# Splitting POOL's lower parts of weights and reordering a pair's end in the last MLP of a diffusion backbone

## The chip, the cores and the metric

The kernel runs on one core of a Trainium2 chip. The metric is the device time of one execution in microseconds (us), as the median of several runs. Times inside an execution come from one profiled execution; they count from its first instruction.

## The reference

Two layers over 1024 latent tokens and 256 context tokens, model width 1024, all in fp32. Layer 0 mixes tokens with a Conformer convolution module, layer 1 with grouped-query attention; each layer ends in a squared-ReLU MLP. Only the latent tokens are returned, so the MLP of layer 1 runs on 1024 tokens.

```
for i in range(2):
    mod_l = split(silu(c) @ w_mod[i] + b_mod[i], 6)          # shift, scale, gate twice; mod_c alike
    hl, hc = modulate(rms_norm(x, norm1_g[i]), ...), ...
    ol, oc = conv_module(hl), conv_module(hc)   if i == 0    # depthwise convolution of 31 taps
    ol     = gqa_mixer(hl, hc)                  if i == 1    # QK-norm, 2-D rotary, softmax
    xl = xl + mod_l[2] * ol
    hl = modulate(rms_norm(xl, norm2_g[i]), mod_l[3], mod_l[4])
    xl = xl + mod_l[5] * (square(relu(hl @ w_ff1[i])) @ w_ff2[i])    # w_ff1: 1024 x 4096
    ...                                                      # the context likewise in layer 0
return xl
```

## The kernel before

Everything is fp32 in memory. A product is made from split operands: the upper part of a number is its value rounded to the matmul format (fp32r), made by ACT with a copy; the lower part is the value minus its upper part, made by POOL or DVE with a subtraction. Of the four partial products three are kept, so each product of a weight tile and 512 tokens is three matmuls. In `unit`, a 128 x 1024 tile of weights is loaded on SP's queue into a buffer `raw` (three of them), ACT makes its upper part (L205), and POOL (or DVE, where `eng` says so) its lower part in one instruction of 1024 columns (L208).

The language's scheduler places the instructions on the engines. Written order is a preference that `high_priority(n)` moves n instructions ahead; each engine's queue is then worked off strictly in the order in which it was filled, and an instruction that waits holds up what is behind it. A tile with k buffers is handed out again when its last reader is placed before the next writer.

The last MLP (`mlp1`, `ff2`) is written as a Strassen-like scheme with seven products instead of eight for each 2 x 2 block. The token halves and feature halves are combined beforehand into `T1`, `T2`, `T3`, `T4`, `B11`, `B21`, `B22`, each split into upper and lower parts. The 32 column tiles of `w_ff1` are taken as 16 pairs. For pair j, `w1_ops` loads the two raw tiles `ra` and `rb` (L1334, L1335), forms the sums of weights on DVE (L1347 to L1351), splits them (`unit`: L1340 on ACT, L1341 on POOL; `S1`/`S3` in one tile, `S2`/`S4` in another), and splits `A22` on its own (L1354, L1355). All of this is called up 115 instructions ahead for pairs 0 to 7 and 190 for pairs 8 to 15 (`AH1`). There is one buffer for `A22`'s parts.

The loop over pairs then issues on TensorE, twelve matmuls a product (L1186):

- for pairs 8 to 15 A11·B11 into bank b1; for pairs 0 to 7 this and A12·B21 were done before the loop (while the norm was going on) and come back from memory as p1 and s11;
- S1·T1 into b5, copied to p5 (L1376); S3·T3 into b7, copied to p7 (L1380); POOL adds p7 to p5 (L1381); S2·T2 into b6, added to p1 (L1384), and POOL adds p1 to p5 (L1385);
- for pairs 8 to 15 A12·B21 on top of b1, and its hidden values;
- S4·B22 on top of b5: these matmuls add into the bank from which L1376 has copied, so they wait for that copy;
- A22·T4 on top of b7, likewise after L1380.

p1 and p5 lie in a ring of four slots, two for even and two for odd pairs. Then comes the pair's end, which this text calls its tail: the hidden values (ReLU and square, L1299 and L1300, with a store to scratch memory `hd`) of p5; s12 from b5 and p1 (L1395 to L1397); T1 (L1401), T2 (L1403 on POOL), T3 (L1405); p1 from b7 (L1408) and its hidden values; T4 (L1411). T1 to T4 are stored to `hd` by L1400. In the code the part of the tail that needs only S4 stands between S4 and A22, the rest behind A22. `ff2` reads `hd` back and does the second matrix in the same scheme; its `unit` (L1429 ACT, L1430 POOL or DVE) splits 1024 columns at once too.

L251 is the matmul that sums squares over partitions for a norm; it needs DVE's L284, the last addition of the squares.

Of the kernel before, what the change touches and what calls it, by code (L numbers as in the profile page):

```python
# [11 lines left out]
F32 = mybir.dt.float32  # L12
F32R = mybir.dt.float32r
BF16 = mybir.dt.bfloat16
AF = mybir.ActivationFunctionType
ALU = mybir.AluOpType
# [4 lines left out]
P = 128  # L21
# [47 lines left out]


B = [4.0, 3.64, 3.4, 3.6, 0.41]

AHEAD = [80, 60, 130]
UHP = 100
# [45 lines left out]
NPRO = 8  # L120
AH1, AH2 = (115, 190), 200
PB = 2.5
OPS = ("B11", "B21", "T1", "T3", "T2", "B22", "T4")


class Kern:
# [62 lines left out]
    def unit(self, src, eng=None):  # L189

        nc = self.nc
        cols = lambda ts: lambda c, n=1: ts[c * len(ts) // 8][:, c * P % (1024 // len(ts)):][:, :n * P]
        with self.tc.high_priority(self.ahead):
            raw = self.t("raw", [P, 1024], "raw")
            nc.sync.dma_start(out=raw, in_=src)
            self.nu += 1
            if self.six and self.nu % 6 == 0:
                parts = [[self.t(t, [P, 1024 // len(ts)], "wx", F32R) for t in ts] for ts in self.six]
            else:
                w = self.t("w8", [P, 2, 1024], "wsp", F32R)  # L200
                parts = [[w[:, 0]], [w[:, 1]]]
            hi, lo = [cols(ts) for ts in parts]
            n = 8 // len(parts[0])
            for c in range(0, 8, n):
                nc.scalar.activation(hi(c, n), raw[:, c * P:(c + n) * P], AF.Copy)  # L205
            n = 8 // len(parts[1])
            for c in range(0, 8, n):
                (eng or nc.gpsimd).tensor_tensor(lo(c, n), raw[:, c * P:(c + n) * P], hi(c, n).bitcast(F32), ALU.subtract)  # L208
        return hi, lo
# [212 lines left out]
    def mlp(self, i, X, h, N, segs, gates, budget, hook=None, done=None, eng=None, off=False, each=None,  # L422
# [3 lines left out]
        for c in range(NF // CH):  # L426
# [17 lines left out]
            for m2, mn in MGS:  # L444
# [6 lines left out]
                for z in range(mn):  # L451
# [9 lines left out]
                    if done and c == NF // CH - 1:  # L461
                        done(m)
                    self.pump(budget * B[4])
            if hook:
# [156 lines left out]
    def layer0(self):  # L621
# [21 lines left out]
        self.bg = [n1[1], conv[0]]  # L643
        self.pw1(0, B[0], each=lambda: next(pm, None))
        self.drain(n1[1])
        self.bg.insert(0, n1[2])
        self.pw1(1, B[1], each=lambda: next(pm, None))
        self.drain(n1[2])
        n2 = {}

        def mid(ct):
# [3 lines left out]
            if ct == FRONT:  # L655
# [3 lines left out]
                self.bg.insert(0, n2[-1])  # L659
        self.pw1(2, B[2], mid, each=lambda: next(pm, None))  # L660
        self.drain(n2[-1])
# [527 lines left out]
    def stats1(self, X, box):  # L1189
        yield from self.sumsq(lambda k: X[:, k], 512, box, True)  # L1190

    def mlp1(self, at, pre, r0):
        nc = self.nc
        self.ahead, self.six, self.wide = AHEAD[2], None, True
# [46 lines left out]
        for m in range(KT):  # L1241
# [3 lines left out]
            else:  # L1245
                w = self.unit(self.A["wo"][m])
# [50 lines left out]
        def hidden(c, s, j, o):  # L1297

            nc.scalar.activation(s, c, AF.Relu)  # L1299
            nc.scalar.activation(s, s, AF.Square)  # L1300
            nc.sync.dma_start(out=self.hd[OPS.index(o), :, j], in_=s)
# [7 lines left out]
        for j in range(NPRO):  # L1309
            a11, a12 = halves(self.unit(self.A["w1"][1, 2 * j]))  # L1310
            b1 = self.ps("mm", "b1")
            p1 = self.t("tmp", [P, 512], "p1")
# [16 lines left out]
        ring = [work[:, 4 + i] for i in range(4)]  # L1329

        def w1_ops(j):
            with self.tc.high_priority(AH1[j >= NPRO]):
                ra, rb = [self.t("raw", [P, 1024], "raw") for _ in range(2)]
                nc.sync.dma_start(out=ra, in_=self.A["w1"][1, 2 * j])  # L1334
                nc.sync.dma_start(out=rb, in_=self.A["w1"][1, 2 * j + 1])  # L1335
                u = {}

                def unit(names, src, eng):
                    w = self.t("w8", [P, 2, 1024], "wsp", F32R)
                    nc.scalar.activation(w[:, 0], src, AF.Copy)  # L1340
                    eng.tensor_tensor(w[:, 1], src, w[:, 0].bitcast(F32), ALU.subtract)  # L1341
                    for i, n in enumerate(names):
                        u[n] = tuple(lambda k, y=y, i=i: w[:, y, i * 512 + k * P:i * 512 + k * P + P] for y in range(2))
                if j >= NPRO:
                    unit(("A11", "A12"), ra, nc.gpsimd)
                s = lambda i, n=1: work[:, i:i + n].rearrange("p i n -> p (i n)")
                nc.vector.tensor_tensor(s(0), rb[:, 0:512], rb[:, 512:1024], ALU.add)  # L1347
                nc.vector.tensor_tensor(s(1), ra[:, 0:512], rb[:, 0:512], ALU.subtract)
                unit(("S1", "S3"), s(0, 2), nc.gpsimd)
                nc.vector.tensor_tensor(s(2), s(0), ra[:, 0:512], ALU.subtract)  # L1350
                nc.vector.tensor_tensor(s(3), ra[:, 512:1024], s(2), ALU.subtract)  # L1351
                unit(("S2", "S4"), s(2, 2), nc.gpsimd)
                a = self.t("p1", [P, 2, 512], "a22", F32R)
                nc.scalar.activation(a[:, 0], rb[:, 512:1024], AF.Copy)  # L1354
                nc.vector.tensor_tensor(a[:, 1], rb[:, 512:1024], a[:, 0].bitcast(F32), ALU.subtract)  # L1355
                u["A22"] = tuple(lambda k, y=y: a[:, y, k * P:k * P + P] for y in range(2))
            return u

        def bank(i, name):
            return self.ps(("mm", "mm", "mm", "mm", "cv", "cv", "st", "rb")[i], name)  # L1360

        for j in range(NP):
            u = w1_ops(j)
            q = 4 * (j % 2)
            pro = j < NPRO
            p1 = ring[2 * (j % 2)]
            if pro:
                nc.sync.dma_start(out=p1, in_=self.p1d[:, j])
            else:
                b1 = bank(q, "b1")  # L1370
                self.prod(b1, u["A11"], piece("B11"), True)
                nc.scalar.activation(p1, b1, AF.Copy)  # L1372
            b5 = bank(q + 1, "b5")
            self.prod(b5, u["S1"], piece("T1"), True)
            p5 = ring[2 * (j % 2) + 1]
            nc.scalar.activation(p5, b5, AF.Copy)  # L1376
            b7 = bank(q + 2, "b7")
            self.prod(b7, u["S3"], piece("T3"), True)
            p7 = self.t("acc", [P, 512], "p7")
            nc.scalar.activation(p7, b7, AF.Copy)  # L1380
            nc.gpsimd.tensor_tensor(p5, p5, p7, ALU.add)  # L1381
            b6 = bank(q + 3, "b6")
            self.prod(b6, u["S2"], piece("T2"), True)
            nc.vector.tensor_tensor(p1, b6, p1, ALU.add)  # L1384
            nc.gpsimd.tensor_tensor(p5, p5, p1, ALU.add)  # L1385
            s11 = self.t("tmp", [P, 512], "s11")
            if pro:
                nc.sync.dma_start(out=s11, in_=self.hd[OPS.index("B11"), :, j])
            else:
                self.prod(b1, u["A12"], piece("B21"), False)  # L1390
                hidden(b1, s11, j, "B11")
            self.prod(b5, u["S4"], piece("B22"), False)
            hidden(p5, p5, j, "B22")
            s12 = self.t("tmp", [P, 512], "s12")
            nc.vector.tensor_tensor(s12, b5, p1, ALU.add)  # L1395
            nc.scalar.activation(s12, s12, AF.Relu)  # L1396
            nc.scalar.activation(s12, s12, AF.Square)  # L1397
            t1 = self.t("tmp", [P, 512], "t1")
            t2 = self.t("tmp", [P, 512], "t2")
            out = lambda o, s: nc.sync.dma_start(out=self.hd[OPS.index(o), :, j], in_=s)  # L1400
            nc.vector.tensor_tensor(t1, s12, s11, ALU.subtract)  # L1401
            out("T1", t1)
            nc.gpsimd.tensor_tensor(t2, p5, t1, ALU.subtract)  # L1403
            out("T2", t2)
            nc.vector.tensor_tensor(s12, p5, s12, ALU.subtract)  # L1405
            out("T3", s12)
            self.prod(b7, u["A22"], piece("T4"), False)
            nc.vector.tensor_tensor(p1, b7, p1, ALU.add)  # L1408
            hidden(p1, p1, j, "B21")
            t4 = self.t("tmp", [P, 512], "t4")  # L1410
            nc.vector.tensor_tensor(t4, p1, t2, ALU.subtract)  # L1411
            out("T4", t4)
        self.ff2(X)

    def ff2(self, X):


        nc = self.nc
# [7 lines left out]
        def unit(src, eng):  # L1426

            w = self.t("pc", [P, 2, 1024], "u", F32R)
            nc.scalar.activation(w[:, 0], src, AF.Copy)  # L1429
            eng.tensor_tensor(w[:, 1], src, w[:, 0].bitcast(F32), ALU.subtract)  # L1430
            return w

        def add(acc, bank, c):
# [8 lines left out]
        def out(blk, m, x, b):  # L1442

            y = self.t("acc", [P, 512], "y")
            nc.vector.scalar_tensor_tensor(y, b, g[:, m:m + 1], x, ALU.mult, ALU.add)  # L1445
            nc.sync.dma_start(out=self.out[:, m, blk * 512:blk * 512 + 512], in_=y)
# [9 lines left out]
        for c in range(NC):  # L1456
            last = c == NC - 1
# [5 lines left out]
            for what, y, first in ending if last else order:  # L1463
                with self.tc.high_priority(AH2):
                    tu, wu = [], []
                    z = {"B11": 0, "B21": 1, "T4": 3}.get(what)
                    for i in range(2):
                        f = self.t("raw", [P, 1024], "tf")
                        nc.sync.dma_start(out=f.rearrange("p (i n) -> p i n", i=2),
                                          in_=self.hd[OPS.index(what), :, c * CP2 + 2 * i:c * CP2 + 2 * i + 2])  # L1470
                        tu.append(unit(f, V if i else G))
                    for i in range(2):
                        h = slice(1024 * i, 1024 * i + 1024)
                        s = S[:, h]
# [155 lines left out]
```

## Time and profile before

| what | value |
|---|---|
| median of 3 runs | 2923.48 us (2922.95 to 2928.18) |
| profiled execution | 2921.92 us, its span 2920.1 us, granted clock 0.981 |
| PE (TensorE matmuls) | 2759.9 us busy, 95% of the span |
| DVE | 2046.4 us, 70% |
| POOL | 1568.6 us, 54% |
| ACT | 1481.9 us, 51% |
| DMA | 406.66 MB, mean 139 GB/s |

A row of a timeline gives start, duration, engine, line, operation, output and inputs, how many instructions are merged, and in brackets the idle time just before and what ended it. A row of waits gives who waited for whom, the sum in us, how often, and the longest. A row of windows gives the stretch, its length, the busy time (and count) of PE, PEld (weight loads), DVE, ACT and POOL, the granted clock, the DMA share and GB/s. A row of an instruction's line gives the shortest, median and longest duration in ns. SPq is the queue on which loads and stores are issued.

### The profile page before, as it was taken

To read this page: it belongs to the slowest core of one execution; us is meant where nothing else is said; L and a number is where in the kernel's file an instruction comes from. 1 tells how busy PE (TensorE), PEld (TensorE's weight loads), DVE (VectorE), ACT (ScalarE), POOL (GpSimd) and SP (SyncE) were. 2 spreads that over 40 slices of the span, in tenths; PEclk is the share of its full clock that TensorE was granted. 3 is DMA by queue.
4 is the path that set the end of the run, shared out by engine and by line. 5 is a ranking of instruction groups with operands and counts; after the bars stand their busy time and mean duration, and the time that the engine had idled before them with its cause. 6 is when DMAs were issued, how large, how long until landed. Compare 5 with 4: busy or idle time off the path is not lost. (4 is left out here: it accounts for less than half of the span.)

```text
span 2920.1 us, 35997 instructions
## 1 busy us (share of the span) xinstructions
PE 2759.9 (95%) x12634; PEld 2320.2 (79%) x12634; DVE 2046.4 (70%) x3268; ACT 1481.9 (51%) x2386; POOL 1568.6 (54%) x915
## 2 busy tenths in 40 slices
PE   7999999999989999989998899999999888999999
PEld 2778999999888999978886677776767767888887
DVE  3888998987565432455358899976986645558797
ACT  4553554546444354536344576755675544454332
POOL 3777666676456564444334566644666555553221
PEclk9999999999999999999999999999999899999999
DMA  7554333343876534434344411132106454465452
GB/s 239 171 175 160 125 120 115 109 140 120 269 244 202 196 114 157 130 125 141 119 147 144 127 23 22 23 98 61 22 15 217 147 177 160 150 239 190 159 177 101
DMA packets 176580, 406.66 MB, mean 139 GB/s; under 512 B 21328, under 2 KB 64848, under 8 KB 174352
## 3 DMA queue, kind: packets, MB, share of 16 engines
q1 hardware_dynamic: 176400, 404.37, 42.9%
q8 instruction: 99, 1.62, 0.2%
q14 instruction: 81, 0.66, 0.1%
HBM read 343.49 MB, written 60.82 MB: 138 GB/s over the span
## 5 line engine op out<-in xcount | busy, mean ns | idle before, releaser
L208 POOL TENSOR_TENSOR wsp<-raw,wsp 128x1024 fp32r<-128x1024 f32 x254 | 616.8, 2438 | 447.0 <-ACT wsp L205 405.5
L216 PE MATMUL ps<-h,wsp 128*128 128x432 f32 (+1 forms) x2832 | 574.4, 361 | 5.0 <-ACT h L316 2.9
L216 PEld LDWEIGHTS ps<-h,wsp 128*128 128x128 f32 x2832 | 533.3, 189 | 44.4 <-issue 10.1
L205 ACT ACTIVATE wsp<-raw 128x1024 fp32r<-128x1024 f32 x291 | 306.0, 1056 | 316.8 <-PE ps L216 202.7
L554 DVE SCALAR_TENSOR_TENSOR cv<-u,vec,cv 128x464 f32<-128x464 f32 (+2 forms) x696 | 422.7, 669 | 4.8 <-ACT cv L551 3.3
L216 PE MATMUL ps<-hb,wsp 128*128 128x432 f32 (+1 forms) x1920 | 400.4, 363 | 20.1 <-DVE X L459 11.3
L216 PEld LDWEIGHTS ps<-hb,wsp 128*128 128x128 f32 x1920 | 364.1, 191 | 41.6 <-issue 14.6
L1081 POOL TENSOR_TENSOR p<-e,p 128x512 fp32r<-128x512 f32 x223 | 306.6, 1388 | 164.9 <-ACT p L1079 99.5
L1186 PE MATMUL b<-u 128*128 128x512 f32 x1344 | 305.4, 389 | 0.0
L1186 PEld LDWEIGHTS b<-u 128*128 128x128 f32 x1344 | 252.1, 188 | 53.2 <-DVE sums L1437 0.4
L1074 ACT ACTIVATE e<-sT 128x512 f32<-128x512 f32 x320 | 185.8, 595 | 125.3 <-PE sT L1072 105.0
L1036 DVE TENSOR_REDUCE m<-s 128x1 f32<-128x512 f32 (+1 forms) x336 | 191.8, 590 | 11.5 <-PE s L1034 10.0
L1430 POOL TENSOR_TENSOR u<-tf,u 128x1024 fp32r<-128x1024 f32 x28 | 76.7, 2738 | 174.3 <-ACT u L1429 174.3
L459 DVE SCALAR_TENSOR_TENSOR X<-ps,m,X 128x432 f32<-128x432 f32 (+2 forms) x144 | 81.3, 586 | 118.5 <-PE ps L216 118.3
L361 DVE CUSTOM_DVE_ANT_0 rawh<-rawh,scp 128x512 f32<-128x512 f32 x128 | 86.5, 684 | 103.0 <-DMA rawh<-in_wmod 95.6
L1077 DVE CAST p<-e 128x512 fp32r<-128x512 f32 x160 | 116.0, 726 | 31.0 <-ACT e L1074 26.9
L437 DVE TENSOR_TENSOR hb<-ps,hb 128x432 fp32r<-128x432 f32 (+1 forms) x96 | 57.4, 598 | 111.6 <-ACT ps L436 111.4
L1186 PE MATMUL b<-T,wsp 128*128 128x512 f32 x576 | 133.6, 389 | 0.4 <-POOL wsp L1341 0.4
L1088 PE MATMUL O<-p,half 128*128 128x512 f32 x320 | 127.4, 398 | 0.0
L1186 PEld LDWEIGHTS b<-T,wsp 128*128 128x128 f32 x576 | 108.1, 188 | 23.4 <-POOL wsp L1341 0.8
L216 PE MATMUL ps<-h,wx 128*128 128x432 f32 (+1 forms) x624 | 125.4, 356 | 0.0
L208 POOL TENSOR_TENSOR wx<-raw,wx 128x1024 fp32r<-128x1024 f32 x45 | 109.1, 2424 | 27.6 <-ACT wx L205 26.1
(314 smaller groups left out, 5388.6 us busy)
## 6 DMA issues: line engine op xcount, KB each, us to landing
raw<-in_w SPq DMA_DIRECT2D x232, 512.0 KB, 3.4
raw<-in_pw SPq DMA_DIRECT2D x72, 512.0 KB, 3.4
rawh<-in_wmod SPq DMA_DIRECT2D x128, 256.0 KB, 3.6
tf<-hd SPq DMA_DIRECT2D x56, 512.0 KB, 4.0
raw<-in_qkv SPq DMA_DIRECT2D x36, 512.0 KB, 3.3
rawp<-in_wmod SPq DMA_DIRECT2D x32, 512.0 KB, 4.4
raw<-in_w2s SPq DMA_DIRECT2D x16, 1024.0 KB, 7.2
hd<-t SPq DMA_DIRECT2D x48, 256.0 KB, 2.3
```

Source lines behind the costliest of these rows:

```text
L205: nc.scalar.activation(hi(c, n), raw[:, c * P:(c + n) * P], AF.Copy)
L208: (eng or nc.gpsimd).tensor_tensor(lo(c, n), raw[:, c * P:(c + n) * P], hi(c, n).bitcast(F32), ALU.subtract)
L216: self.nc.tensor.matmul(ps, lhsT=(wh, wl, wh)[t], rhs=(ah, ah, al)[t], start=first and i == t == 0, stop=last and i == n - 1 and t == 2)
L361: nc.vector.tensor_tensor_reduce(raw, raw, scp[z], 1.0, 0.0, ALU.mult, ALU.add, accum_out=part[:, z, u:u + 1])
L459: nc.vector.scalar_tensor_tensor(X[:, m, a:a + n], pss[z][:, a:a + n], gates[cc][:, m:m + 1], X[:, m, a:a + n], ALU.mult, ALU.add)
L554: nc.vector.scalar_tensor_tensor(dst, src, tap, acc[z][:, :N], ALU.mult, ALU.add)
L1036: nc.vector.reduce_max(m3[:, qt, j, c:c + 1], s[:, :w], axis=AX.X)
L1074: nc.scalar.activation(e, s, AF.Exp, scale=0.125)
L1077: nc.vector.tensor_copy(p[:, 0], e)
L1081: (nc.vector if u % lm == lm - 1 else nc.gpsimd).tensor_tensor(p[:, 1], e, p[:, 0].bitcast(F32), ALU.subtract)
L1088: nc.tensor.matmul(O[1], lhsT=self.half, rhs=p[:, 0], start=a, stop=False)
L1186: self.nc.tensor.matmul(ps, lhsT=w[t % 2](k), rhs=(ah, ah, al)[t], start=first and k == t == 0, stop=k == 3 and t == 2, skip_group_check=True)
```

## The change

It has four parts. `PLN = 4` makes POOL's lower part in `unit` two instructions of 512 columns instead of one of 1024; DVE's stay whole. A new function `lower` does the same in `w1_ops` and in `ff2`. The raw loads of `w1_ops` are called up 90 instructions further ahead than the rest of it. The tail becomes a function that is called in the next pair, behind the copies p5 and p7 of that pair (the last pair's after the loop); in it L1408's operation stands right behind s12's addition, and A22·T4 follows S4·B22 directly.

```
+PLN = 4
...
-            n = 8 // len(parts[1])
+            n = min(8 // len(parts[1]), 8 if eng else PLN)
             for c in range(0, 8, n):
                 (eng or nc.gpsimd).tensor_tensor(lo(c, n), raw[...], hi(c, n).bitcast(F32), ALU.subtract)
...
+    def lower(self, eng, w, src):
+        n = 512 if eng is self.nc.gpsimd else 1024
+        for i in range(0, 1024, n):
+            eng.tensor_tensor(w[:, 1, i:i + n], src[:, i:i + n], w[:, 0, i:i + n].bitcast(F32), ALU.subtract)
...
         def w1_ops(j):
-            with self.tc.high_priority(AH1[j >= NPRO]):
+            ah = AH1[j >= NPRO]
+            with self.tc.high_priority(ah + 90):
                 ra, rb = [self.t("raw", [P, 1024], "raw") for _ in range(2)]
                 nc.sync.dma_start(out=ra, in_=self.A["w1"][1, 2 * j])
                 nc.sync.dma_start(out=rb, in_=self.A["w1"][1, 2 * j + 1])
+            with self.tc.high_priority(ah):
...
-                    eng.tensor_tensor(w[:, 1], src, w[:, 0].bitcast(F32), ALU.subtract)
+                    self.lower(eng, w, src)                  # in ff2's unit as well
...
+        def tail(j, p1, p5, s11, b5, b7):
+            hidden(p5, p5, j, "B22")
+            s12 = self.t("tmp", [P, 512], "s12")
+            nc.vector.tensor_tensor(s12, b5, p1, ALU.add)
+            nc.vector.tensor_tensor(p1, b7, p1, ALU.add)
+            nc.scalar.activation(s12, s12, AF.Relu)
+            nc.scalar.activation(s12, s12, AF.Square)
+            hidden(p1, p1, j, "B21")
+            ...                                              # T1, T2, T3, T4 and their stores, as before
+        last = None
         for j in range(NP):
...
             nc.scalar.activation(p7, b7, AF.Copy)
+            if last:
+                tail(*last)
             nc.gpsimd.tensor_tensor(p5, p5, p7, ALU.add)
...
             self.prod(b5, u["S4"], piece("B22"), False)
-            hidden(p5, p5, j, "B22")
-            ...                                              # s12, T1, T2, T3
             self.prod(b7, u["A22"], piece("T4"), False)
-            ...                                              # p1, its hidden values, T4
+            last = j, p1, p5, s11, b5, b7
+        tail(*last)
         self.ff2(X)
```

More of the change, by code (lines that the diff above doesn't have):

```diff
@@ L1360, in bank @@
             return self.ps(("mm", "mm", "mm", "mm", "cv", "cv", "st", "rb")[i], name)
+        def tail(j, p1, p5, s11, b5, b7):
[6 more added lines that the diff above has]
+            hidden(p1, p1, j, "B21")
+            t1 = self.t("tmp", [P, 512], "t1")
+            t2 = self.t("tmp", [P, 512], "t2")
+            out = lambda o, s: nc.sync.dma_start(out=self.hd[OPS.index(o), :, j], in_=s)
+            nc.vector.tensor_tensor(t1, s12, s11, ALU.subtract)
+            out("T1", t1)
+            nc.gpsimd.tensor_tensor(t2, p5, t1, ALU.subtract)
+            out("T2", t2)
+            nc.vector.tensor_tensor(s12, p5, s12, ALU.subtract)
+            out("T3", s12)
+            t4 = self.t("tmp", [P, 512], "t4")
+            nc.vector.tensor_tensor(t4, p1, t2, ALU.subtract)
+            out("T4", t4)
+        last = None
         for j in range(NP):
@@ L1392, in mlp1 @@
             self.prod(b5, u["S4"], piece("B22"), False)
-            hidden(p5, p5, j, "B22")
[L1394 to L1406, printed above, removed]
-            self.prod(b7, u["A22"], piece("T4"), False)
[L1408 to L1412, printed above, removed]
+            self.prod(b7, u["A22"], piece("T4"), False)
+            last = j, p1, p5, s11, b5, b7
+        tail(*last)
         self.ff2(X)
@@ L1429, in unit @@
             nc.scalar.activation(w[:, 0], src, AF.Copy)
-            eng.tensor_tensor(w[:, 1], src, w[:, 0].bitcast(F32), ALU.subtract)
+            self.lower(eng, w, src)
             return w
```

## The prediction

> **What bounds the kernel now.** I read the busy shares first, then who TensorE waited for, then the windows of the stage that is edited, then its timeline.
>
> ```profile
> PE 2759.9 (95%) x12634; PEld 2320.2 (79%) x12634; DVE 2046.4 (70%) x3268; ACT 1481.9 (51%) x2386; POOL 1568.6 (54%) x915
> ...
> PE b L1186 <- ACT work L1376: 20.0, 7, 6.2
> PE st L251 <- DVE acc L284: 14.3, 7, 5.8
> PE pa L216 <- POOL wsp L208: 0.8, 1, 0.8
> PE b L1186 <- POOL wsp L1341: 0.4, 1, 0.4
> ...
> 2317.20:2453.20 136.00, 115.96 (x468) 92.39 (x469) 65.52 (x83) 58.96 (x89) 77.52 (x41) 0.94 0.54 177
> 2455.90:2592.00 136.10, 135.80 (x591) 110.59 (x590) 68.34 (x74) 67.56 (x106) 77.83 (x42) 1.00 0.46 148
> 2701.00:2774.00 73.00, 73.00 (x324) 60.45 (x323) 57.72 (x54) 26.62 (x26) 18.73 (x8) 1.00 0.46 159
> ```
>
> TensorE is busy 2759.9 of 2920.1 us, so all waits together are 160 us. The largest single one, 20.0 us in seven times, is the first half of the last MLP's pair loop (pairs 0 to 7, 2317 to 2453 us): PE 115.96 of 136.00 us at clock 0.94. The second half (pairs 8 to 15) has 135.80 of 136.10 at 1.00, and ff2 73.00 of 73.00: nothing is to be had there. POOL's lower parts of weights, which the change cuts in two everywhere, are waited for directly in 0.8 + 0.4 us.
>
> ```profile
> 2317.22 8.25 PE L1186 MATMUL b<-T,wsp 128*128 128x512 f32 x35 [0.40 <-POOL wsp L1341]
> ...
> 2360.01 4.61 PE L1186 MATMUL b<-u,wsp 128*128 128x512 f32 x12 [4.60 <-ACT work L1376]
> ...
> 2376.84 3.07 PE L1186 MATMUL b<-u,wsp 128*128 128x512 f32 x12 [1.25 <-ACT work L1376]
> ...
> 2393.47 4.51 PE L1186 MATMUL b<-u,wsp 128*128 128x512 f32 x12 [2.57 <-ACT work L1376]
> ...
> 2448.23 5.07 PE L1186 MATMUL b<-u,wsp 128*128 128x512 f32 x12 [6.18 <-ACT work L1376]
> ...
> 2455.94 2.88 PE L1186 MATMUL b<-B,wsp 128*128 128x512 f32 x12
> ...
> 2469.54 2.97 PE L1186 MATMUL b<-u,wsp 128*128 128x512 f32 x12
> ```
>
> Pairs 0 to 7 take 2455.94 - 2317.22 = 138.7 us. Undisturbed, 591 matmuls take 135.8 us (window above), 0.230 each, and a pair of the first half has 60: 13.8 us, eight of them 110.3. So 28 us are lost here: 20.0 waiting, the rest in matmuls that run slowly after a wait (4.61, 4.51 and 5.07 us for twelve against 2.97). Each wait is before S4 of a pair, which adds into the bank that the copy L1376 must read first. Why L1376 is late, over one period (pair 2 ends, pair 3 waits, pair 4 is prepared; one pair's share of each engine):
>
> ```profile
> 2359.59 0.41 SPq L1335 DMA_DIRECT2D raw<-in_w  x1
> ...
> 2364.27 0.69 DVE L1347 TENSOR_TENSOR work<-raw 128x512 f32<-128x512 f32 x1 [4.01 <-DMA raw<-in_w]
> ...
> 2365.59 1.06 ACT L1340 ACTIVATE wsp<-work 128x1024 fp32r<-128x1024 f32 x1 [5.15 <-DVE work L1348]
> 2366.20 0.69 DVE L1351 TENSOR_TENSOR work<-raw,work 128x512 f32<-128x512 f32 x1
> 2366.73 2.43 POOL L1341 TENSOR_TENSOR wsp<-work,wsp 128x1024 fp32r<-128x1024 f32 x1 [4.93 <-ACT wsp L1340]
> 2366.81 0.68 DVE L1384 TENSOR_TENSOR work<-b,work 128x512 f32<-128x512 f32 x1
> 2366.92 0.33 SPq L1334 DMA_DIRECT2D raw<-in_w  x1
> ...
> 2369.12 1.29 POOL L1385 TENSOR_TENSOR work<-work 128x512 f32<-128x512 f32 x1
> ...
> 2370.45 0.63 ACT L1299 ACTIVATE work<-work 128x512 f32<-128x512 f32 x1 [2.46 <-POOL work L1385]
> ...
> 2372.96 0.69 DVE L1401 TENSOR_TENSOR t<-s,s 128x512 f32<-128x512 f32 x1 [4.69 <-ACT s L1397]
> ...
> 2374.30 0.68 DVE L1408 TENSOR_TENSOR work<-b,work 128x512 f32<-128x512 f32 x1
> 2374.90 1.18 DVE L1355 TENSOR_TENSOR a<-raw,a 128x512 fp32r<-128x512 f32 x1
> 2375.01 0.63 ACT L1299 ACTIVATE work<-work 128x512 f32<-128x512 f32 x1 [1.56 <-DVE work L1408]
> ...
> 2376.21 0.58 ACT L1376 ACTIVATE work<-b 128x512 f32<-128x512 f32 x1
> ...
> 2376.44 0.40 SPq L1335 DMA_DIRECT2D raw<-in_w  x1
> ```
>
> This is a closed cycle of 2376.44 - 2359.59 = 16.85 us, longer than the 13.8 that TensorE needs: raw load 4.68, sums and upper part, L1341 2.4, L1385 1.3, the hidden values on ACT 2.5, the tail's subtractions on DVE, L1355, which gives the raw buffer back, and the next load. The PE waits are this cycle showing through at L1376.
>
> **The tail behind the next pair's copies.** Program order would give: L1376 and L1380 of pair j+1 stand on ACT ahead of pair j's L1299, S4 no longer waits. Against it stands an order in the rows: L1384 at 2366.81 belongs to pair 2, whose S2 was done before 2360.01, yet it stands behind L1347 to L1351 of pair 4, written two pairs later and called up 115 instructions, about 1.2 pairs. So engines do not take this program in written order nor by priority alone: what was expected to be ready first goes first. Without a delay, pair j's L1408 is ready as soon as A22 is done and its L1299 needs ACT for 1.3 us, while L1376 of j+1 is ready twelve matmuls later (0.230 x 12 = 2.8). By that the tail still stands in front of L1376. Bounds: 0, if nothing moves; 27 (20.0 waiting and 7 of the slow matmuls), if the copies move ahead everywhere. Also the cycle does not run through L1376, so with the copies ahead pairs are still prepared every 16.9 us, with one pair's lead to use up. I take the low end for this edit alone.
>
> The slow matmuls follow waits of 2.57 us and more (4.51 us for twelve), not that of 1.25 (3.07). The Trainium skill (TensorE: Matmul & The Clock Gate, section "What's actually happening") has the clock halve after about 3.4 us of idling. The rows at 4.60 and 6.18 agree, the one at 2.57 does not; by the page the waits under 3.4 us would cost no clock, and the upper bound would be an estimated 24, not 27. I keep the rows' 27.
>
> The last pair's tail has no next pair: it stands after A22, so its first half is later by up to one product (2.8 us); ff2 begins with 96 matmuls (22 us) that do not need it. The second half of the loop has no wait, so a moved tail gains nothing there; what covers it is a rival below.
>
> **Raw weights 90 instructions further ahead.** The row of L1334 shows when a load goes: at 2366.92, as L1351 has ended (2366.20 + 0.69 = 2366.89) and its buffer is free. L1335 goes after L1355 (2374.90 + 1.18 = 2376.08) at 2376.44, 0.36 later, behind a store on SP. Three raw buffers set the time, not the priority; only that 0.36 can go. Six pairs: 2.2 us; ends 0 and 2.2. On SP a load put ahead of stores makes them wait for its buffer; they feed scratch memory that ff2 reads over 100 us later. Before the loop, pair 0's two loads now go ahead of the last first-half unit's:
>
> ```profile
> 2283.40 0.43 SPq L1335 DMA_DIRECT2D raw<-in_w  x1
> ...
> 2289.84 1.04 ACT L205 ACTIVATE wsp<-raw 128x1024 fp32r<-128x1024 f32 x1
> ```
>
> If that unit's load took the later place, 2283.40, it would land by 2283.40 + 4.68 = 2288.1, before its L205 at 2289.84: nothing, with 1.8 us of cover.
>
> **POOL's lower parts in halves.** A half costs what L1385 costs, 1.29, so a unit costs 2 x 1.29 - 2.43 = 0.15 more on POOL.
>
> ```profile
> 2347.54 4.80 POOL L1341 TENSOR_TENSOR wsp<-work,wsp 128x1024 fp32r<-128x1024 f32 x2 [4.39 <-ACT wsp L1340]
> 2352.31 1.28 POOL L1385 TENSOR_TENSOR work<-work 128x512 f32<-128x512 f32 x1
> ...
> 69.58 2.74 DVE L284 TENSOR_TENSOR acc<-acc,acc 128x432 f32<-128x432 f32 x1 [1.01 <-POOL acc L282]
> ...
> 69.50 2.36 POOL L208 TENSOR_TENSOR wsp<-raw,wsp 128x1024 fp32r<-128x1024 f32 x1
> ...
> L208 POOL TENSOR_TENSOR wsp<-raw,wsp x254: 2342/2406/4581, 46.5 to 2291.7; 128x1024 fp32r<-128x1024 f32 x127
> ```
>
> In the cycle: L1385 is ready at 2367.5 (L1384 ends) and waits for the whole L1341. After a half it starts at 2366.73 + 1.29 = 2368.0 instead of 2369.12: 1.1 a pair, seven pairs 7.8. In pairs like the one at 2347.54 it stands behind two whole L1341, 4.80; with more seams I take one half more there, for two of the seven: 2.5. Ends for the halves: -1 (L1385 still behind all, 0.15 each) and 7 x 2.4 = 17. I take 10 and with the load 12 us for the stage.
>
> Elsewhere: L284 starts 0.08 after POOL's L208 and ends 0.46 after it: the two exclude each other for whole instructions. With a half the lock goes at 70.8, L284 ends 1.1 earlier. TensorE waits for L284 in seven places: ends 0 and 7.7; I take 4, since in some of them POOL is elsewhere. Cost: 254 of L208's x 0.15 = 38 us on an engine with 1350 us free. TensorE feels a late POOL where it waits anyway, 160 of 2920 us: 38 x 0.055 = 2; ends 0 and twice that. I take 2. In ff2 PE at 73.00 of 73.00 hides it; if that cover went, 0.15 for each of its lower parts.
>
> **Sum.** -12 - 4 + 2 = -14 from the profiled 2921.92 us (span 2920.1 and 1.8 around it): 2907.9. The median of the runs, 2923.48, is 1.6 above: 2909.5, so 2909.
>
> **Rivals.** (a) The copies do go ahead of the tail. For it: L1299 and L1376 are ready within some 2 us of each other. Then the stage loses its 27 us, less 2 at the first pairs; with 2 net outside: 2923.5 - 25 - 2 = 2896. (b) The change doesn't do what it says: order as before, L1385 behind both halves, the gain at L284 eaten by POOL's cost. For it: the loads are bound by buffers and orders by readiness. 2923. (c) Slower: the tail falls too far back in pairs 8 to 15, where nothing waits now.
>
> ```profile
> 2474.59 0.63 ACT L1299 ACTIVATE work<-work 128x512 f32<-128x512 f32 x1 [7.64 <-POOL work L1385]
> ...
> 2483.54 0.63 ACT L1300 ACTIVATE work<-work 128x512 f32<-128x512 f32 x1
> ...
> 2485.98 0.60 ACT L1380 ACTIVATE p<-b 128x512 f32<-128x512 f32 x1
> ```
>
> Pair 8's tail takes 2483.54 + 0.63 - 2474.59 = 9.6 us on ACT. Behind pair 9's L1380 it would end at 2485.98 + 0.60 + 9.6 = 2496.2. Its slot in the ring is written again by pair 10's first copy, which A12 of pair 10 needs: that pair starts at 2455.94 + 2 x 19.3 (84 matmuls of 0.230 each) = 2494.5, and A12 comes 48 matmuls (11.0) later, at 2505.5. That leaves 9 us. If three whole lower parts (7.3) and a raw load (4.7) get in front of the tail, TensorE waits 3 us in each of seven pairs: +21, and the stage's 12 are not won: 2923.5 + 21 - 2 = 2942. It decides from 9 us of delay on. Against it: POOL is busy there only 77.83 of 136.10, and no pair of this half waits now.
>
> **How the numbers follow.** Chances: forecast (the cycle shortened, 2902 to 2917) 0.44, (a) 0.26, (b) 0.17, (c) 0.13. 0.2% is 5.8 us, about what this measurement can tell: faster 0.70, same 0.17, slower 0.13. The range takes in (a) with 4 us to spare and leaves out most of (c) and a tenth for what no row shows: 2892 to 2930.
>
> **What would show it.** Right: L1385 between halves of L1341; seven or so waits of S4 on L1376, smaller, together 8 to 13 us; a cycle of 15 to 15.7 us from L1335 to L1335; the wait on L284 near 10 us; L1334 still at the end of L1351; POOL's busy time up by 40 us or more. Wrong: no wait on L1376 at all, rival (a); L1385 after both halves, (b); PE waits between 2456 and 2592, (c); or new waits before 2300 us, where every engine's order may shift with several hundred added instructions.

## The result, and the profile after

The changed kernel takes 2905.90 us (median of 4 runs, 2902.28 to 2907.84) against 2925.82 us of the kernel before on the same chip: a ratio of 0.9932, 95% interval 0.9920 to 0.9944, or 19.9 us less (16.4 to 23.4). The forecast was 2909. The time is as forecast; the places it came from are not.

Line numbers after the change: L1376 is now L1409 and L1380 is L1413 (copies p5, p7), L1341 is L1198 (in `lower`), L1340 is L1350, L1385 is L1420, L1384 is L1419, L1347 to L1351 are L1357 to L1361, L1354/L1355 are L1364/L1365, L1334/L1335 are L1343/L1344, L1299/L1300 are L1307/L1308, L1401 is L1384, L1403 is L1386, L1405 is L1388, L1408 is L1377, L208 is L210, L251 is L253, L284 is L286. The page's busy line and two rows of TensorE's waits, as shown of before:

```profile
PE 2752.6 (95%) x12634; PEld 2314.2 (80%) x12634; DVE 2005.7 (69%) x3268; ACT 1483.5 (51%) x2386; POOL 1657.6 (57%) x1286
...
PE b L1188 <- ACT work L1409: 15.6, 7, 3.2
...
PE st L253 <- DVE acc L286: 12.8, 5, 5.6
```

POOL, with 1286 instructions instead of 915, is busier by 89 us; DVE, with the same 3268, is less busy by 41. TensorE runs the same 12634 matmuls in 7.3 us less, so half of the span's 14.2 us (2920.1 to 2905.9) is not waiting that went but matmuls that ran at a faster clock (granted 0.981 before, 0.985 after).

Where the time came from is read from windows cut at the same matmuls in both kernels: 251 matmuls of layer 1's k and q, 639 from the end of attention to the first pair, pairs 0 to 7 (480, counted as 482 and 481 with those at the edges), and the rest. Columns as in the prediction's windows. First before, then after:

```profile
1276.20:1344.20 68.00, 53.06 (x251) 43.05 (x250) 52.52 (x91) 28.67 (x52) 27.75 (x15) 0.97 0.44 135
2141.30:2316.43 175.13, 160.35 (x639) 123.65 (x638) 124.70 (x142) 110.79 (x180) 103.61 (x59) 0.94 0.44 141
2316.43:2455.94 139.51, 119.09 (x482) 94.58 (x480) 68.16 (x87) 59.73 (x90) 78.25 (x42) 0.94 0.53 174
2455.94:2918.00 462.06, 460.00 (x2017) 377.94 (x2015) 342.78 (x337) 191.25 (x234) 171.82 (x78) 1.00 0.50 167
```

```profile
1278.50:1343.10 64.60, 51.38 (x251) 41.80 (x250) 48.09 (x91) 28.86 (x52) 30.45 (x23) 1.00 0.47 142
2136.50:2307.97 171.47, 157.77 (x639) 121.62 (x638) 115.92 (x142) 110.42 (x179) 107.15 (x76) 0.96 0.45 142
2307.97:2440.70 132.73, 117.04 (x481) 93.05 (x480) 64.72 (x84) 59.98 (x90) 83.16 (x61) 0.96 0.55 182
2440.70:2903.70 463.00, 459.48 (x2017) 378.19 (x2015) 327.65 (x341) 191.41 (x234) 206.36 (x130) 1.00 0.49 168
```

The pair loop's first half gives 6.8 us, the two stages ahead of it 3.4 and 3.7, and the rest costs 0.9. The starts of the windows give what lies between them: nothing is gained up to the first, which the changed kernel reaches 2.3 us later (1278.50 against 1276.20), and between the first and the second it gains 3.7. In the two stages ahead DVE does the same 91 and 142 instructions in 4.4 and 8.8 us less, while POOL is busier. (From the first T product, at 2316.43, to 2317.22 is counted with the pairs here; the prediction's 138.7 leaves it out.)

One period of pairs 0 to 7 after, from raw load to raw load:

```profile
2367.22 0.40 SPq L1344 DMA_DIRECT2D raw<-in_w  x1
...
2371.57 0.69 DVE L1357 TENSOR_TENSOR work<-raw 128x512 f32<-128x512 f32 x1 [3.68 <-DMA raw<-in_w]
...
2374.04 2.56 POOL L1198 TENSOR_TENSOR wsp<-work,wsp 128x512 fp32r<-128x512 f32 x2 [4.60 <-ACT wsp L1350]
...
2376.57 1.28 POOL L1420 TENSOR_TENSOR work<-work 128x512 f32<-128x512 f32 x1
...
2377.88 0.63 ACT L1307 ACTIVATE work<-work 128x512 f32<-128x512 f32 x1 [2.59 <-POOL work L1420]
...
2380.40 0.69 DVE L1384 TENSOR_TENSOR t<-s,s 128x512 f32<-128x512 f32 x1 [4.81 <-ACT s L1379]
...
2381.73 0.68 DVE L1377 TENSOR_TENSOR work<-b,work 128x512 f32<-128x512 f32 x1
2382.33 1.18 DVE L1365 TENSOR_TENSOR a<-raw,a 128x512 fp32r<-128x512 f32 x1
2382.45 0.63 ACT L1307 ACTIVATE work<-work 128x512 f32<-128x512 f32 x1 [1.56 <-DVE work L1377]
...
2383.65 0.58 ACT L1409 ACTIVATE work<-b 128x512 f32<-128x512 f32 x1
...
2383.89 0.41 SPq L1344 DMA_DIRECT2D raw<-in_w  x1
```

It is the old order of the queues. L1420 stands behind both halves, not between them; the tail's hidden values (L1307) still stand on ACT in front of the copy L1409, though the code now calls them behind it; the period is 2383.89 - 2367.22 = 16.67 us against 16.85. Over six periods the mean is (2418.05 - 2314.73) / 6 = 17.22 us against (2429.76 - 2323.16) / 6 = 17.77 before.

### The profile page after: what moved, and what is told of

Same layout as the page of the kernel before. It is cut to its first block, busy times and chain, and to the rows that moved or that the text cites. A ratio compares the mean times of both kernels' runs of the same rounds, so it can differ in the third digit from the quotient of the medians.

```text
span 2905.9 us, 36468 instructions
## 1 busy us (share of the span) xinstructions
PE 2752.6 (95%) x12634; PEld 2314.2 (80%) x12634; DVE 2005.7 (69%) x3268; ACT 1483.5 (51%) x2386; POOL 1657.6 (57%) x1286
## 5 line engine op out<-in xcount | busy, mean ns | idle before, releaser
L210 POOL TENSOR_TENSOR wsp<-raw,wsp 128x512 fp32r<-128x512 f32 x508 | 662.0, 1332 | 411.2 <-ACT wsp L207 370.2
L1198 POOL TENSOR_TENSOR u<-tf,u 128x512 fp32r<-128x512 f32 x56 | 101.5, 1833 | 150.3 <-ACT u L1447 136.1
L210 POOL TENSOR_TENSOR wx<-raw,wx 128x512 fp32r<-128x512 f32 x90 | 115.6, 1307 | 24.9 <-ACT wx L207 24.4
```

Of the source, the lines that this page charges most:

```text
L1198: eng.tensor_tensor(w[:, 1, i:i + n], src[:, i:i + n], w[:, 0, i:i + n].bitcast(F32), ALU.subtract)
```

## The experiments

Twelve kernels, in three groups that each shared a chip with runs of the kernel before (medians 2925.66, 2926.38 and 2924.55 us). "Pairs 0 to 7" is the time from the first T product to pair 8's first product in the profiled execution; undisturbed it would be 110.3.

| run | median us | ratio to before, 95% interval | pairs 0 to 7, us | waits on p5's copy |
|---|---|---|---|---|
| before | 2924.55 to 2926.38 | 1 | 139.5 | 20.0 in 7 |
| changed kernel | 2905.90 | 0.9932 (0.9920 to 0.9944) | 132.7 | 15.6 in 7 |
| e1 halves in `unit` | 2910.69 | 0.9940 (0.9926 to 0.9954) | 139.5 | 18.2 in 6 |
| e2 halves in the pairs | 2921.30 | 0.9979 (0.9970 to 0.9988) | 137.4 | 17.8 in 8 |
| e3 tail and raw loads | 2919.70 | 0.9984 (0.9974 to 0.9994) | 135.0 | 18.0 in 7 |
| e4 all halves | 2908.83 | 0.9937 (0.9923 to 0.9950) | 136.1 | 21.8 in 8 |
| e5 changed, tail tied | 2884.10 | 0.9860 (0.9841 to 0.9878) | 115.7 | 3.3 in 2 |
| e6 changed, two A22 | 2911.55 | 0.9946 (0.9933 to 0.9959) | 133.1 | 16.1 in 8 |
| e7 both | 2902.62 | 0.9910 (0.9892 to 0.9928) | 129.5 | 13.5 in 6 |
| e8 quarters | 2942.11 | 1.0050 (1.0035 to 1.0065) | 137.8 | 18.4 in 8 |
| e9 before, tail tied | 2901.90 | 0.9926 (0.9912 to 0.9939) | 115.8 | 1.9 in 2 |
| e10 as e5, no raw lead | 2887.48 | 0.9868 (0.9851 to 0.9886) | 115.6 | 3.1 in 2 |
| e11 changed, no tail | 2900.71 | 0.9916 (0.9902 to 0.9930) | 134.2 | 15.8 in 7 |
| e12 as e5, pair 8 later | 2882.05 | 0.9854 (0.9840 to 0.9867) | 112.6 | 1.6 in 2 |

**Which part brings the gain: e1 to e4.** e1:

```
+PLN = 4
-            n = 8 // len(parts[1])
+            n = min(8 // len(parts[1]), 8 if eng else PLN)
```

> Before, with PLN = 4 alone (POOL's lower parts in `unit` in halves; last MLP untouched). Theory H (halves bring the gain, by shorter locks and earlier first halves): 6 to 12 us under before, in the norm waits on L284 and in layer 1's q/k/v stage (1280 to 1640 us); the last MLP's pairs 0 to 7 still take 138 to 139 us. Rival T (the tail and the raw loads bring the gain): within 3 us of before. Rival C (the halves cost POOL time that TensorE feels): 2 to 4 us above before.

e2 (in `w1_ops` alone):

```
-                    eng.tensor_tensor(w[:, 1], src, w[:, 0].bitcast(F32), ALU.subtract)
+                    self.lower(eng, w, src)
```

> Before, with the lower parts of `w1_ops` alone in halves. Theory H: pairs 0 to 7 take about 133 us instead of 138.7, because p5's last addition no longer stands behind two whole lower parts; time 4 to 8 us under before. Rival T: pairs 0 to 7 stay at 138 to 139 us, time within 3 us of before. My forecast's own step (the addition slips between the halves): 127 to 129 us for the pairs, 10 us under before.

e3:

```
+            with self.tc.high_priority(ah + 90):     # the two raw loads
...
+            if last:
+                tail(*last)                          # behind the copy p7
```

> Before, with the moved tail and the raw loads 90 further ahead, all lower parts whole. Theory H: within 3 us of before; ACT's hidden values of the pair before still stand in front of the copies p5 and p7, raw loads still go when their buffers come free. Rival T: 10 to 20 us under before, pairs 0 to 7 in 133 us or less.

e4 is e1, e2 and `lower` in `ff2` together:

> Before, with all lower parts of POOL in halves (`unit`, `w1_ops`, `ff2`), tail and raw loads as before. Theory H: 14 to 20 us under before, the same as the full change within 3 us. Rival T: within 4 us of before.

The halves alone (e4) give 18.4 us of the 19.9, and those of `unit` alone (e1) 17.6 us with pairs 0 to 7 unchanged at 139.5: theory H's account of which part brings the gain holds for e1 and e4 (for e1 it had 6 to 12 us, so too little), and e1's gain lies outside the last MLP. (e1's profiled execution, 2917.11 us, is the slowest of its five, so its trace doesn't show where all of the 17.6 us lie.) That the halves do it by shorter waits of DVE is argued from the windows above, where TensorE waits for DVE; no run shows it by itself, and e8 below shows that it isn't the whole account. e2 gives 6.1 us, of which the pairs show 2.1, less than either account had. e3 gives 4.7 us (1.8 to 7.6), where theory H had 3 at most. One thing in its trace differs clearly: the wait in pair 7 is 4.21 us, where the four kernels without the raw lead (before, e1, e2, e4) have 5.25 to 6.23. The moved tail isn't needed for it: e11 below, with the lead and the tail where it was, has 2.73. That it is the lead's doing isn't shown: e6 and e7 below have the lead, and their waits in pair 7 are 5.30 and 5.35. (Gains here are one minus the ratio times 2925.66; further down they are differences of medians.) The single parts add up to 28 us, so they are not independent.

**What sets pairs 0 to 7: e5 to e7.** The changed kernel's tail moved only in the code, not in the queues. e5 ties it:

```
-            nc.scalar.activation(p7, b7, AF.Copy)
+            cp = nc.scalar.activation(p7, b7, AF.Copy)
             if last:
-                tail(*last)
+                with self.tc.issue_after(cp.ins):
+                    tail(*last)
```

> The changed kernel, with the tail's instructions tied behind the copy p7 of the next pair, so that on ACT the copies p5 and p7 really stand in front of the hidden values of the pair before. Theory Y (the closed cycle through the one A22 buffer and the raw buffer sets pairs 0 to 7; the copies show it, they don't make it): the waits on p5's copy go, waits on `S1`/`S3` or `A22` weights take their place, pairs 0 to 7 take 128 to 135 us, time within 5 us of the changed kernel. Rival A (the copies standing behind the tail are the cause, as in my rival (a)): no wait is left, pairs 0 to 7 take 112 to 116 us, 15 to 20 us under the changed kernel.

e6 gives A22's tile a second buffer:

```
-    ... "p1": 1}
+    ... "p1": 2, "onesd": 1, "half": 1}      # two constants move from their own pool to make room
```

> The changed kernel, with two buffers for A22's parts (room made by giving two constants buffers of another pool). The raw tile `rb` no longer waits for A22's product of the pair before until it is free, so the cycle is open. Theory Y: raw loads go several us earlier, the period of pairs 0 to 7 falls from 16.9 to 14 to 15 us, pairs 0 to 7 take 112 to 122 us, 10 to 20 us under the changed kernel. Rival A: waits on p5's copy stay (12 us or more), within 4 us of the changed kernel.

> Both of the above together. Theory Y: as with two A22 buffers alone or up to 5 us better, 110 to 118 us for pairs 0 to 7. Rival A: as with the tail tied alone. If both causes act in series, only this one reaches 112 us and the others stay near 130.

My theory Y fell. Tying the tail took pairs 0 to 7 from 132.7 to 115.7 us, as rival A had it, and the time to 2884.1, 21.8 us under the changed kernel where rival A had 15 to 20. The second A22 buffer brought nothing by itself (133.1 us for the pairs) and cost some 15 to 18 us beside the tied tail (by the ratios and by the medians). One period of e5:

```profile
2336.25 0.33 SPq L1344 DMA_DIRECT2D raw<-in_w  x1
...
2340.92 0.69 DVE L1357 TENSOR_TENSOR work<-raw 128x512 f32<-128x512 f32 x1 [4.10 <-DMA raw<-in_w]
...
2347.24 5.98 POOL L1198 TENSOR_TENSOR wsp<-work,wsp 128x512 fp32r<-128x512 f32 x4
...
2348.49 0.60 ACT L1409 ACTIVATE work<-b 128x512 f32<-128x512 f32 x1 [3.19 <-DMA hd<-work]
2349.13 0.60 ACT L1413 ACTIVATE p<-b 128x512 f32<-128x512 f32 x1
2349.16 0.69 DVE L1376 TENSOR_TENSOR s<-b,work 128x512 f32<-128x512 f32 x1 [1.32 <-PE b L1188]
2349.62 0.62 ACT L1307 ACTIVATE work<-work 128x512 f32<-128x512 f32 x1
...
2349.76 1.04 DVE L1365 TENSOR_TENSOR a<-raw,a 128x512 fp32r<-128x512 f32 x1
...
2350.73 0.68 DVE L1377 TENSOR_TENSOR work<-b,work 128x512 f32<-128x512 f32 x1
2350.84 0.33 SPq L1344 DMA_DIRECT2D raw<-in_w  x1
```

The copies now stand in front of L1307, and on DVE L1365, which gives the raw buffer back, stands in front of the tail's L1377. The period is 2350.84 - 2336.25 = 14.59 us instead of 16.67 (the mean of six is 14.52). The links that fell out are the tail's own: hidden values, then DVE's subtractions and L1377, then L1365; of the tail only s12's addition (L1376) still stands right ahead of L1365. They had made the cycle long, and moving the tail moves them. The tie moved both orders at once, the copies on ACT and L1365 on DVE; no run moves one alone, so what each is worth isn't shown. POOL's four halves of a pair now run as one stretch, and TensorE waits for none of them; what is left are two waits on p5's copy, 1.41 and 1.89 us, in pairs 6 and 7.

Why the second buffer didn't help, from e6:

```profile
2377.43 0.68 DVE L1377 TENSOR_TENSOR work<-b,work 128x512 f32<-128x512 f32 x1
2377.53 3.12 SPq L1383 DMA_DIRECT2D hd<-t  x2
2378.03 1.15 DVE L1365 TENSOR_TENSOR a<-raw,a 128x512 fp32r<-128x512 f32 x1
2378.14 0.63 ACT L1307 ACTIVATE work<-work 128x512 f32<-128x512 f32 x1 [0.85 <-DVE work L1377]
2378.59 1.72 POOL L1386 TENSOR_TENSOR t<-work,t 128x512 f32<-128x512 f32 x1
...
2380.75 0.38 SPq L1344 DMA_DIRECT2D raw<-in_w  x1
```

L1365 still stands behind L1377 on DVE, so an A22 buffer that is free earlier is of no use; and the raw buffer is free at 2378.03 + 1.15 = 2379.18, but its load goes at 2380.75, behind stores of the tail that wait on SP for L1386. Why e7 is worse than e5 I did not settle: its order on DVE differs from e5's in many places.

**Smaller pieces: e8.**

```
-PLN = 4
+PLN = 2
-        n = 512 if eng is self.nc.gpsimd else 1024
+        n = 256 if eng is self.nc.gpsimd else 1024
```

> The changed kernel, with POOL's lower parts in quarters (256 columns) instead of halves. Theory H (the gain outside the last MLP comes from shorter stretches in which POOL keeps DVE out): DVE's busy time falls again by 10 to 30 us, POOL's rises by 80 to 150 us, time 2 to 8 us under the changed kernel. Rival S (the gain came from the lower part's first half being ready sooner for TensorE or from a chance shift of the orders): DVE's busy time stays, time from 2 us under to 15 us above the changed kernel.

DVE's busy time fell by another 22 us (2005.7 to 1983.4) and POOL's rose by 152 (to 1809.5), about as theory H has it, yet the kernel is 36 us slower than with halves and 16 slower than before. Neither theory had that. So DVE's busy time is no measure of the gain; in e9 below it is even higher than before (2073.1 against 2046.4), and the kernel is faster. Part of the loss has a place, layer 0's convolution, where a copy of 248 columns on DVE (L503, L501 before) stands beside POOL's lower parts. It comes twice in an execution. The first time, before, after, and with quarters:

```profile
158.58 4.82 POOL L208 TENSOR_TENSOR wsp<-raw,wsp 128x1024 fp32r<-128x1024 f32 x2
158.66 2.47 DVE L501 COPY u<-halo 128x248 f32<-128x248 f32 x1
```

```profile
159.82 5.03 POOL L210 TENSOR_TENSOR wsp<-raw,wsp 128x512 fp32r<-128x512 f32 x4
159.91 5.09 DVE L503 COPY u<-halo 128x248 f32<-128x248 f32 x1 [0.37 <-POOL halo L526]
```

```profile
160.13 5.60 POOL L210 TENSOR_TENSOR wsp<-raw,wsp 128x256 fp32r<-128x256 f32 x8
160.21 8.43 DVE L503 COPY u<-halo 128x248 f32<-128x248 f32 x1 [1.52 <-POOL halo L526]
...
165.69 2.80 POOL L210 TENSOR_TENSOR wx<-raw,wx 128x256 fp32r<-128x256 f32 x4
```

The second time, after and with quarters (before, it took 0.29 us, ahead of POOL's lower parts):

```profile
267.56 8.90 POOL L210 TENSOR_TENSOR wsp<-raw,wsp 128x512 fp32r<-128x512 f32 x7
267.65 1.37 DVE L503 COPY u<-halo 128x248 f32<-128x248 f32 x1 [0.49 <-POOL halo L526]
```

```profile
272.38 11.22 POOL L210 TENSOR_TENSOR wsp<-raw,wsp 128x256 fp32r<-128x256 f32 x16
272.48 11.26 DVE L503 COPY u<-halo 128x248 f32<-128x248 f32 x1 [1.34 <-POOL halo L526]
```

The copy takes 0.29 us when alone. It got in behind the first whole lower part (2.47 us) and, the second time, behind the first half (1.37 us); but it passed over three seams between halves (5.09 us), eleven between quarters (8.43 us) and fifteen (11.26 us). What decides at a seam isn't shown. TensorE's first 1201 matmuls, which take in both places, are done at 298.2 us before, at 301.2 with halves and at 312.8 with quarters. So 11.6 of the 36 us are lost by then; the rest comes later and is not traced here.

**What the tied tail needs: e9, e10, e11, e12.** e9 ties the tail in the kernel before; e10 is e5 with `high_priority(ah)` instead of `ah + 90` for the raw loads; e11 is the changed kernel with the tail where it was; e12 is e5 with `AH1` at (115, 115) instead of (115, 190).

> Before, with the tail moved and tied behind the next pair's copy p7; lower parts whole, raw loads as before. Theory Z (the tail's own instructions, standing in front of L1355 on DVE and of the copies on ACT, were the links that made the cycle 16.9 us; out of the way the cycle is about 14.5 us): pairs 0 to 7 take 114 to 122 us, time 17 to 24 us under before. Rival W (the short cycle needs the halves or the earlier raw loads as well): 128 us or more for the pairs, time 0 to 12 us under before.

> The tail tied behind p7, halves as in the changed kernel, raw loads called up with the rest of `w1_ops` (the 90 taken away). Theory: raw loads are bound by their buffers, so pairs 0 to 7 stay within 2 us of the 115.7 us of the tied kernel with the 90, and the time within 3 us of its 2884. Rival: with the tail out of the way the loads are bound by priority; pairs 0 to 7 take 120 us or more, 5 to 15 us above 2884.

> The changed kernel without the moved tail (halves and raw loads stay). Theory (as written, the moved tail doesn't change the steady order of the queues): within 3 us of the changed kernel, pairs 0 to 7 in 132 to 136 us with waits on p5's copy of 15 us or more. Rival: the moved tail is worth what halves alone lack, so 4 to 8 us above the changed kernel.

> The tail tied behind p7 as in the tied kernel, and the weights of pairs 8 to 15 called up 115 instead of 190 instructions ahead, so that pair 8's upper parts no longer stand between the copies of pair 7. Theory: the two waits left in pairs 6 and 7 (1.41 and 1.89 us, with 1.5 us of slow matmuls) go or shrink, 1 to 5 us under 2884. Rival: pair 8's weights come late instead, TensorE waits for its first product, 2 to 10 us above 2884.

The windows of pairs 0 to 7 in e9 and in e12:

```profile
2319.16:2434.93 115.77, 111.69 (x482) 89.84 (x480) 76.09 (x79) 57.26 (x90) 82.21 (x41) 1.00 0.59 194
```

```profile
2307.37:2419.93 112.56, 110.97 (x481) 89.98 (x480) 69.94 (x79) 57.67 (x91) 81.81 (x58) 1.00 0.61 200
```

Theory Z's forecast holds: the tied tail needs neither halves nor earlier loads (e9: 115.8 us, clock 1.00, 22.7 us under before). The tie in the last MLP (22.7) and the halves (18.4) together make the 41 to 42 us of e5 (2926.38 - 2884.10 = 42.3). The raw lead shows no worth once the tail is tied (e10: 115.6 us; 2887.5 against 2884.1, intervals overlapping). Without the moved tail the changed kernel is not slower (e11: 0.9902 to 0.9930 against 0.9920 to 0.9944); it was a move in the code alone. In e12 the wait in pair 7 is gone, and 112.6 us for the pairs is 2.3 above undisturbed. e12 and e5 are the fastest kernels here, 43 and 42 us under before; the 2 us between them are within their intervals.

## Why the prediction was right, and where it was not

The sum was right by two errors that cancel, and that is luck. It had 12 us in the pairs and 2 outside; the profiled executions give 6.8 and 7.4, the runs with halves alone 18 with most of it outside. Of the six signs named for it two came, L1334's successor at the end of L1361 and POOL's busy time. Four did not: L1420 is not between the halves, the waits on p5's copy are 15.6 us and not 8 to 13, the period is above 15.7 us, and the wait on L286 is 12.8 us and not near 10. In the pairs the order is that of rival (b), which had no gain.

- **Tail at 0:** right for the change as written (e11), and for the reason given: the queues are filled by readiness, and the order did not move. **The bound behind it was right, the argument about the cycle wrong.** The step "with the copies ahead pairs are still prepared every 16.9 us" failed: the cycle was listed there with L1299, L1401 and L1408 in it, all parts of the tail that the same edit would move. Tied, the period is 14.59 us. Rival (a)'s price was 27 less 2; the tie brought 22.7 (e9).
- **Raw loads:** L1343 goes at 2374.23, as L1361 ends, and L1344 0.38 us after L1365 ends (2383.51): buffers set the time, as said. The 2.2 us for the gap of 0.36 were not won; the gap is still there. What the lead does besides, at pair 7 for one (e3), isn't settled.
- **Halves in the cycle, 10 us:** the step that failed is "after a half it starts". POOL takes up L1420 behind both halves of a unit, in each of the first seven pairs of the changed kernel. In e4 it came between the halves of a unit in two pairs, behind one half of four in one and behind three in the other; so the step is possible, but not the rule. What was won came from other things: the pair that stood behind two whole lower parts (4.80 us) stands behind one unit's halves (2.6), waits of TensorE on p5's copy fell by 4.4 us, and some 2 us are matmuls at a faster clock.
- **L284, 4 us:** the mechanism is right, for the instruction that was costed to the hundredth; the size of the term is not.

```profile
L284 DVE TENSOR_TENSOR acc<-acc,acc x13: 557/2159/2832, 22.7 to 2258.2; 128x432 f32<-128x432 f32 x5, 128x416 f32<-128x416 f32 x3, 128x384 f32<-128x384 f32 x2, 128x512 f32<-128x512 f32 x2
```

```profile
69.93 2.85 POOL L210 TENSOR_TENSOR wsp<-raw,wsp 128x512 fp32r<-128x512 f32 x2
70.01 1.65 DVE L286 TENSOR_TENSOR acc<-acc,acc 128x432 f32<-128x432 f32 x1 [2.35 <-POOL acc L284]
...
L286 DVE TENSOR_TENSOR acc<-acc,acc x13: 558/1084/1745, 21.1 to 2252.5; 128x432 f32<-128x432 f32 x5, 128x416 f32<-128x416 f32 x3, 128x384 f32<-128x384 f32 x2, 128x512 f32<-128x512 f32 x2
```

The one costed at 2.74 us, 1.1 less with a half, takes 1.65; the median goes from 2.16 to 1.08. The Trainium skill (SBUF — State Buffer, section "Who interferes with whom") says that a DVE instruction with both inputs in SBUF contends with a POOL instruction that reads SBUF, and calls the pair of ports that they share an exclusive lock; these rows agree. But TensorE's wait on it fell by 1.5 us only (14.3 to 12.8). So the term was 2.5 us too large for this line. What it left out are other instructions of DVE that stand beside POOL's: DVE's busy time, net of some that grew, fell by 41 us in all, 13 of them in the two stages shown, where TensorE waits for DVE. Not every instruction with two inputs is among them: L1384, with one input in the bank b, takes 0.676 to 0.684 us in all 16 cases before, also in the middle of a lower part.
- **POOL's cost:** 89 us instead of 38. On average a unit costs 2 x 1.332 = 2.664 instead of 2.438, 0.23 more and not 0.15 (by the shortest ones, 2 x 1.251 against 2.342, it is 0.16), and 371 instructions were added, not 254: those that write `wx`, `ff2` and the pairs come on top. What TensorE paid for it isn't separable here.
- **Clock:** the seven waits after are 0.72 to 3.21 us, and two of the longest behave unlike each other:

```profile
2367.65 4.61 PE L1188 MATMUL b<-u,wsp 128*128 128x512 f32 x12 [3.08 <-ACT work L1409]
...
2434.97 3.07 PE L1188 MATMUL b<-u,wsp 128*128 128x512 f32 x12 [3.21 <-ACT work L1409]
```

The first wait is shorter and costs 1.5 us of slow matmuls, the second costs none. Over all fourteen traces: of 34 such waits up to 1.81 us none is followed by slow matmuls (over 4 us for twelve), of 32 between 1.88 and 3.29 us 19 are, of 14 from 3.42 us on all. The Trainium skill (TensorE: Matmul & The Clock Gate, section "What's actually happening") has the clock set by a window of about 3.4 us that runs free of the kernel, and lowered after a window of idling. A window that runs free would make the middle group a matter of chance, as these rows have it; but idling for a whole window isn't needed, 1.88 us already cost clock.

## What to carry to other kernels

When a closed cycle is longer than the engine's work, write down which instructions are in it, and ask of each edit which of them it moves; an edit that takes links out shortens the cycle even if it doesn't touch the engine that shows the wait. Where a scheduler fills queues by readiness, moving code says little: look at the order on the engine, and tie the instruction if it hasn't moved (here 22 us that the rewrite left lying). A long instruction on POOL can hold up instructions of DVE beside it for its whole length, so cut it once and measure: halves gave 18 us, while quarters were 36 us slower than halves.

## What the runs showed of the hardware that I had not expected

- A DVE copy of 0.29 us waited through 16 back-to-back POOL instructions of 0.7 us each, 11.26 us in all, though in another trace the same copy got in behind the first of seven halves (1.37 us): cutting POOL's work in pieces doesn't by itself let DVE in at the seams.
- Waits of TensorE between 1.88 and 3.29 us cost clock in 19 of 32 cases and nothing in the others; half of what the changed kernel gained in its profiled execution (7.3 of 14.2 us) was matmuls at a faster clock rather than waiting.
- POOL's subtraction of 1024 columns takes 2.438 us on average as one instruction, 2.664 as two and 4 x 0.773 = 3.092 as four.
